# Retrieval in two rounds, and new places in memory for stationary and moving tiles, in a fused decoder block

## The chip, the cores and the metric

One NeuronCore of a Trainium2 chip runs the whole block as one program. The metric is the time of one execution on the device in microseconds (us); the kernel before takes 1010.98 us, the median of three runs (1010.77 to 1011.91).

## The reference, cut to what matters

256 tokens of width 1024 pass through one decoder layer: an attention part (a block-sparse and a latent branch, merged by gates), then a retrieval mixer (PEER), then a last norm. The change touches the mixer most. Per token and head (8 heads) it does this:

```
q  = (xc @ w_query)                      # 8 heads x 2 halves x 128
s1, s2 = q[:, :, 0] . sub_keys_1, q[:, :, 1] . sub_keys_2     # 128 scores each
v1, i1 = top_k(s1, 16);  v2, i2 = top_k(s2, 16)
cand = v1[..., :, None] + v2[..., None, :]                    # 256 sums
best, pos = top_k(cand, 16);  g = softmax(best)
idx = i1 * 128 + i2 at pos                                    # 16 of 16384 experts
act = gelu(expert_u[idx] . x);   out = sum(g * act * expert_v[idx])
```

The kernel gathers no experts. It multiplies every token with all 16384 rows of `expert_u` (128 groups of 128), multiplies the gelu of that by a matrix of gates that is zero except at the chosen experts, and multiplies the product with all of `expert_v`.

## The kernel before, in words

**Precision.** Every large product is made of three: a float32 operand is split into a rounded part `hi` and a rest `lo`, and TensorE adds hi*hi, hi*lo and lo*hi in PSUM. `emit_split` (lines 123 to 137) splits one weight unit of 128 x 1024: ScalarE writes `hi` (line 133), and GpSimd or VectorE subtracts for `lo` (line 135). Which of the two does so is fixed per unit in `lo_eng` (lines 107 to 110): GpSimd for the query weights and for the first NP = 8 expert groups, VectorE for all later ones. Weights arrive by DMAs of 512 KB on SyncE's queue, four buffers deep; `hi` and `lo` have four buffers each, and a unit is split two units ahead of its use.

**First stage, up to about 205 us.** `mm3` (lines 144 to 147) has activations as stationary operand and weights as moving one, 512 columns at a time in most steps. The stationary tiles are `hTh` and `hTl` (chunks 1 to 7 of the input projection, 4 units each, at 512 columns; chunk 0 has 416), `cTh` and `cTl`, the `yT` tiles (branch products) and `mTh` and `mTl` (output product). They lie in the pool `pb`, one tile after the other, each rounded up to 32 bytes. Byte addresses in a partition, divided by 128: `hTh` 954.75, `hTl` 1146.75, `mTh` 1082.75, `mTl` 1018.75, `cTh` 1236, `cTl` 1260, the four `yT` 1286 to 1382 (all even). The weight tiles `hi` and `lo` and the tiles `ah` and `al` of the last stage lie in other pools, all at odd whole numbers. `posi`, `posf` and `st` are small tiles of `pb` that stand ahead of these in the order of addresses (`posi` ahead of `hTh`, `posf` ahead of `cTh`, the four `st` ahead of the probability tiles `p` and `pt`).

**Queries and retrieval, about 205 to 365 us.** In 16 rounds `query(n)` makes a query half and `scores(n-1)` its 128 scores for both token halves; `top16` (lines 786 to 797) finds the 16 largest with VectorE's searches. From round 11 on, a generator (`retrieval`, lines 891 to 909) puts one piece of further work into VectorE's order at each call of `next(work)`. It treats four blocks (token half, head half) one after the other, each in full: sums of candidates (line 801), two searches of 80 candidates, `gate_in` and `decode`, `gate_exp` on ScalarE and `pick_keys` (lines 850 and 853, bf16 elements, 2048 of each partition), `gate_norm` and `fold_keys` (bf16 sums, line 858). When a block of the first token half is folded, `post` issues 64 indirect DMAs on GpSimd's queue that scatter its gates to DRAM. Between the calls `more_u(1)` puts one expert group (`u_block`, 24 matmuls of 256 columns, lines 737 to 739) into TensorE's order. Engines run their instructions in the order written.

**Wide expert steps, about 365 to 651 us.** `u_wide` (lines 747 to 754) does an expert group by 8 pairs: a matmul of 512 columns (`hi` against both parts of the activations, line 752) and one of 256 (`lo`, line 753). The activations are `h2`, with all blocks of the high part first and then all of the low part, so the 512 columns are two runs of 256 that lie 8 KB apart. Per pair of tokens a one-hot product (line 991) builds gates of the second token half. 35 groups are done narrow before this loop, 85 wide in it, and 8 narrow after it; results for the second token half are put into DRAM by `spill` until the gates are there.

**Last stage, 651 to 995 us.** Line 1075: the gated activations `ah` and `al` are stationary, the `expert_v` units move, 512 columns at a time.

Of the kernel before, what the change touches and what calls it, by code (L numbers as in the profile page):

```python
# [11 lines left out]
F32 = mybir.dt.float32  # L12
F32R = mybir.dt.float32r
BF = mybir.dt.bfloat16
U32 = mybir.dt.uint32
I32 = mybir.dt.int32
AF = mybir.ActivationFunctionType
OP = mybir.AluOpType
AX = mybir.AxisListType

P = 128
T = 256
NT = 2
D = 1024
ND = 8
H = 8
# [16 lines left out]
def block_kernel(ctx, tc, consts, constb, pos, x, g_mix, g_ffn, g_fin, w_in, g_q, w_qup, g_kv, w_kvup,  # L43
                 w_ba, w_bb, w_out, w_pq, keys, exp_u, exp_v, out):
    nc = tc.nc
    V, S, G, PE = nc.vector, nc.scalar, nc.gpsimd, nc.tensor
    ctx.enter_context(tc.manual_schedule())
    per = ctx.enter_context(tc.tile_pool(name="per", bufs=1))
# [104 lines left out]
    iota = per.tile([P, P, NB], BF, name="iota")  # L153
    small = per.tile([P, 64], F32, name="small")
    nc.gpsimd.memset(small[:, 63:64], -0.5)
    h2 = per.tile([P, 2, ND, T], F32R, name="h2")
    h2h, h2l = h2[:, 0], h2[:, 1]
    x2d = dram.tile([T, D], F32, name="x2d")
    gd = dram.tile([P * P * P, 1], F32, name="gd")
    gld = dram.tile([P, P, P], F32, name="gld")  # L160
# [40 lines left out]

    spread(0)
    idle(2)
    posi = pb.tile([P, NT], I32, name="posi")
    nc.gpsimd.dma_start(posi, pos)
    gqb = pb.tile([P, 384], F32, name="gqb")
    cb = pb.tile([P, B_I16], BF, name="cb")
# [118 lines left out]
        G.tensor_tensor(dst[:, :, half:], c3[:, :, half:], s3[:, :, :half], op=OP.add)  # L326


    posf = pb.tile([P, NT], F32, name="posf")
    G.tensor_copy(posf, posi)  # L330
    ang = pb.tile([P, NT, 48], F32, name="ang")
    kk = pb.tile([P, NT, 48], F32, name="kk")
# [149 lines left out]
    def att_a(i):  # L482
        q, k, v, h, sc, y = heads[i]
        s = sct()
        PE.matmul(s[:, :256], q[:, 128:], k, start=True, stop=False, skip_group_check=True)  # L485
        PE.matmul(s[:, 256:384], q[:, :128], k[:, :128], start=False, stop=False, skip_group_check=True)
        PE.matmul(s[:, 128:384], identb, maskb, start=False, stop=True, skip_group_check=True)
        st = pb.tile([P, 8], F32, name="st", tag="st", bufs=4)
        V.tensor_reduce(st[:, 0:1], s[:, 256:384], AX.X, OP.max)
        V.tensor_reduce(st[:, 1:2], s[:, :256], AX.X, OP.max)  # L490
        V.tensor_scalar(st[:, 2:4], st[:, 0:2], -sc, None, op0=OP.mult)
        p = pb.tile([P, 384], F32, name="p", tag="p", bufs=2)
        S.activation(p[:, :128], s[:, 256:384], AF.Exp, bias=st[:, 2:3], scale=sc, accum_out=st[:, 4:5])
        S.activation(p[:, 128:], s[:, :256], AF.Exp, bias=st[:, 3:4], scale=sc, accum_out=st[:, 5:6])
        live[i] = (p, st)
# [251 lines left out]
    def u_wide(j):  # L747
        hi, lo = wget(U_U[j])
        s = sct()
        for b in range(ND):  # L750
            bs = slice(b * P, (b + 1) * P)
            PE.matmul(s.rearrange("p (z n) -> p z n", z=2), hi[:, bs], h2[:, :, b, :], start=b == 0, stop=False)  # L752
            PE.matmul(s[:, :T], lo[:, bs], h2h[:, b, :], start=False, stop=b == ND - 1)  # L753
        return s

# [43 lines left out]
    def candidates(b):  # L799
        m, c = mval[b], cand[b]  # L800
        V.tensor_tensor(c[:, :, 0:16], m[:, 0, :, 0:1].to_broadcast([P, HG, 16]), m[:, 1], op=OP.add)
        V.tensor_tensor(c[:, :, 16:16 + 8 * NA].rearrange("p h (a b) -> p h a b", a=NA),
                        m[:, 0, :, 1:1 + NA, None].to_broadcast([P, HG, NA, 8]),
                        m[:, 1, :, None, 0:8].to_broadcast([P, HG, NA, 8]), op=OP.add)
        V.tensor_tensor(c[:, :, 16 + 8 * NA:], m[:, 0, :, 1 + NA:16],
                        m[:, 1, :, 0:1].to_broadcast([P, HG, 8]), op=OP.add)

    def retrieve_top(b, h):
        c, pos = cand[b], bpos[b]
        top16([(best[b][:, h + k, :], pos[:, h + k, :], c[:, h + k, :], rep[k][:, :NCAND]) for k in range(2)])  # L810
# [5 lines left out]
    def gate_in(b):  # L816
        V.tensor_tensor(gates(b).rearrange("p (h k) -> p h k", h=HG), best[b],
                        best[b][:, :, 0:1].to_broadcast([P, HG, 16]), op=OP.subtract)

    def gate_exp(b):  # L820
        S.activation(gates(b), gates(b), AF.Exp)

    def gate_norm(b):

        e = gates(b).rearrange("p (h k) -> p h k", h=HG)
        V.tensor_reduce(gsum, e, AX.X, OP.add)
        V.reciprocal(gsum, gsum)
        V.tensor_tensor(e, e, gsum[:, :, None].to_broadcast([P, HG, 16]), op=OP.mult)

    def decode(b):  # L830
        d = dec
        pf = bpos[b].rearrange("p h k -> p (h k)")
        V.tensor_copy(ix, midx[b].rearrange("p c h k -> p (c h k)")[:, :, None].to_broadcast([P, P, 2]))

        V.tensor_scalar(d[:, 0].bitcast(U32), pf, 3, None, op0=OP.logical_shift_right)
        V.tensor_scalar(d[:, 1].bitcast(U32), pf, 7, None, op0=OP.bitwise_and)
        V.tensor_copy(d[:, 4], pf)
        V.tensor_copy(d[:, 3], d[:, 0].bitcast(U32))
        V.tensor_copy(d[:, 5], d[:, 1].bitcast(U32))
        V.tensor_scalar(d[:, 0], d[:, 3], 1.0, 8.0, op0=OP.is_equal, op1=OP.mult)  # L840
        V.scalar_tensor_tensor(d[:, 5], d[:, 4], 15.5 + 8 * NA, d[:, 5], op0=OP.is_lt, op1=OP.mult)
        V.tensor_scalar(d[:, 3], d[:, 3], -1.0, 0.0, op0=OP.add, op1=OP.max)
        V.tensor_tensor(ab[:, 1].rearrange("p h k -> p (h k)"), d[:, 5], d[:, 0], op=OP.add)
        V.scalar_tensor_tensor(ab[:, 0].rearrange("p h k -> p (h k)"), d[:, 4], -float(8 + 8 * NA), d[:, 3],
                               op0=OP.add, op1=OP.max)

    def pick_keys(b):

        abv = ab.rearrange("p c h k -> p (c h) k")
        V.tensor_tensor(oh, abv[:, :, None, :].to_broadcast([P, H, 16, 16]),  # L850
                        i16b[:, None, :, :].to_broadcast([P, H, 16, 16]), op=OP.is_equal)
        o2 = oh.rearrange("p h a (k z) -> p (h a) k z", z=2)
        V.tensor_tensor(o2, o2, ix[:, :, None, :].to_broadcast([P, P, 8, 2]), op=OP.mult)

    def fold_keys(b):
        n = 8
        while n > 1:
            V.tensor_tensor(oh[:, :, :n], oh[:, :, :n], oh[:, :, n:2 * n], op=OP.add)  # L858
            n //= 2
        o4 = oh.rearrange("p (c h) a k -> p c h a k", c=2)  # L860
        t, g = b
        dst = sel[:, 0:2, g * 64:(g + 1) * 64] if t else ij
        V.tensor_tensor(dst.rearrange("p c (h k) -> p c h k", h=HG), o4[:, :, :, 0], o4[:, :, :, 1], op=OP.add)
        if t == 0:

            V.scalar_tensor_tensor(ij[:, 0], ij[:, 1], float(P), ij[:, 0], op0=OP.mult, op1=OP.add)
            V.tensor_scalar(addr[g], ij[:, 0], float(P), tok, op0=OP.mult, op1=OP.add)
# [4 lines left out]
    def post(g):  # L872


        for h in range(HG):
            own = []
            for k in range(16):
                c = slice(16 * h + k, 16 * h + k + 1)
                i = nc.gpsimd.indirect_dma_start(  # L879
                    out=gd[:, :], out_offset=bass.IndirectOffsetOnAxis(ap=addr[g][:, c], axis=0),  # L880
                    in_=gate[g][:, c], in_offset=None, compute_op=OP.add if g or h else OP.bypass).ins
                nc.gpsimd.nop()
                for m in own:
                    tc.declare_no_dep(i, m, reason="other experts")
                if k == 0:
                    for m in ends:
                        tc.add_manual_dep(i, m.name, SYNC, reason="same tokens, next head")
                own.append(i)
            ends[:] = own

    def retrieval(b):
        candidates(b)
        yield
        for h in range(0, HG, 2):
            retrieve_top(b, h)
            yield
        gate_in(b)
        decode(b)
        yield
        if b[0] == 0:  # L900
            gate_exp(b)
        pick_keys(b)
        yield
        if b[0] == 0:
            gate_norm(b)
        fold_keys(b)
        if b == (0, 1):
            post(1)
        yield

    def all_retrieval():
        for b in ((0, 0), (1, 0), (0, 1), (1, 1)):
            yield from retrieval(b)

    for n in range(2 * H):
        query(n)
        if n:
            scores(n - 1)
        if n == H + 2:
            work = all_retrieval()  # L920
        if n > H + 2:
            next(work)
    done = [0]

    def more_u(n):
        for _ in range(n):
            u_block(done[0])
            done[0] += 1

    more_u(1)  # L930
    next(work)
    scores(2 * H - 1)
    p2.close()

    while done[0] < NP - 2:
        more_u(1)
        next(work)
    post(0)

    def index_T():  # L940
        tr = trt()
# [7 lines left out]
        S.activation(gTh, tr[:, :P], AF.Copy)  # L949
        V.tensor_tensor(gTl, tr[:, :P], gTh.bitcast(F32), op=OP.subtract)  # L950

    while next(work, 0) is None:
        more_u(1 + done[0] % 2)
    for g in range(2):
        gate_exp((1, g))
        gate_norm((1, g))
    more_u(2)
    index_T()
    gate_T()
    more_u(1)  # L960
# [284 lines left out]
```

## Time and profile before

| | us |
|---|---|
| median of three runs (lowest, highest) | 1010.98 (1010.77, 1011.91) |
| the profiled execution | 1008.6 |
| its span, first to last instruction | 1006.8 |
| TensorE busy | 981.7 (98%) |
| TensorE loading weights | 851.4 (85%) |
| VectorE busy | 728.6 (72%) |
| ScalarE busy | 579.4 (58%) |
| GpSimd busy | 364.7 (36%) |

Busy times overlap. Matmuls are pipelined, so the duration of one is longer than the step from its start to the start of the next; the step is what the time is made of. The prediction's views are: the chain that ended last (followed back from the end, at each step to what released it), stretches with busy time and TensorE's granted clock, and instructions in order of time.

### The profile page before, as it was taken

The numbers are of one execution on the slowest core, as the hardware profiler recorded it, in microseconds if no ns is written. First come the engines' busy times: TensorE is split into PE (matmuls) and PEld (weight loads), VectorE is DVE, ScalarE is ACT, GpSimd is POOL, SyncE is SP. The second block draws the span as 40 slices with busy tenths as digits, with TensorE's granted clock in tenths as the row PEclk, the third lists the DMA queues.
The fourth block names the chain that finished last, engine by engine and source line by source line (L and its number), as shares of the span: only waits on it lengthen the run. The fifth ranks groups of instructions, "written<-read, shape, count | busy, mean of one in ns | idle before, by whom it ended". The sixth has DMA issues, their size and how long they took to land.

```text
span 1006.8 us, 16653 instructions
## 1 busy us (share of the span) xinstructions
PE 981.7 (98%) x5505; PEld 851.4 (85%) x5505; DVE 728.6 (72%) x1637; ACT 579.4 (58%) x1155; POOL 364.7 (36%) x247
## 2 busy tenths in 40 slices
PE   9999999999959999999999999999999999999997
PEld 6878888799959998888888888988888888888885
DVE  4745437657987768888888887677777777777775
ACT  4554463444525467887877877555555555555553
POOL 5645451177877787787778200000000000000000
PEclk9999999999979999999999999999999999999999
DMA  6854457454547888788888766698878888878773
GB/s 194 298 189 146 147 189 250 167 202 157 169 117 183 231 191 206 192 201 199 190 203 198 199 202 191 214 267 246 243 238 241 243 243 239 243 242 244 241 224 126
DMA packets 123096, 209.13 MB, mean 208 GB/s; under 512 B 28321, under 2 KB 75569, under 8 KB 122882
## 3 DMA queue, kind: packets, MB, share of 16 engines
q1 hardware_dynamic: 101232, 198.09, 63.6%
q0 software_dynamic: 16976, 0.96, 5.5%
q10 hardware_dynamic: 4802, 9.01, 2.4%
q8 instruction: 44, 0.72, 0.3%
q14 instruction: 42, 0.34, 0.1%
HBM read 189.59 MB, written 18.42 MB: 207 GB/s over the span
## 4 chain that ended last, share of the span: by engine, by line
PE 92%; DVE 5%; POOL 1%; issue 1%; ACT 1%; POOLq 0%; DVEq 0%; ACTq 0%
PE acc L1075 34%; PE sc L752 16%; PE sc L753 8%; PE acc L146 4%; PE acc L145 4%; PE acc L147 4%; PE sc L739 3%; PE sc L737 3%; PE sc L738 3%; PE acc L991 2%; PE sc L774 1%; PE sc L772 1%; PE sc L773 1%; DVE gm L858 1%; PE sc L485 1%
## 5 line engine op out<-in xcount | busy, mean ns | idle before, releaser
L135 DVE TENSOR_TENSOR lo<-raw,hi 128x1024 fp32r<-128x1024 f32 (+1 forms) x279 | 339.7, 1221 | 89.0 <-ACT hi L133 87.9
L133 ACT ACTIVATE hi<-raw 128x1024 fp32r<-128x1024 f32 (+2 forms) x323 | 339.0, 1053 | 12.7 <-PE acc L147 10.8
L752 PE MATMUL sc<-h,hi 128*128 128x512 f32 x680 | 243.2, 398 | 0.0
L879 POOL DMA_INDIRECT gd<-gate,addr x128 | 218.4, 1706 | 64.9 <-issue 36.6
L753 PE MATMUL sc<-h,lo 128*128 128x256 f32 x680 | 191.1, 281 | 0.0
L1126 POOL TENSOR_TENSOR small<-small 128x1 f32<-128x1 f32 x2 | 1.3, 646 | 440.0 <-DVE small L1124 440.0
L1075 PE MATMUL acc<-hi,al 128*128 128x512 f32 x512 | 157.9, 388 | 0.0
L1075 PE MATMUL acc<-lo,ah 128*128 128x512 f32 x512 | 157.8, 388 | 0.0
L1075 PE MATMUL acc<-hi,ah 128*128 128x512 f32 x512 | 157.7, 388 | 0.0
L752 PEld LDWEIGHTS sc<-h,hi 128*128 128x128 f32 x680 | 127.9, 188 | 28.8
L1059 ACT ACTIVATE ah<-gm 128x256 fp32r<-128x256 f32 x128 | 53.4, 418 | 155.8 <-DVE lo L135 147.8
L135 POOL TENSOR_TENSOR lo<-raw,hi 128x1024 fp32r<-128x1024 f32 x44 | 107.2, 2447 | 69.0 <-ACT hi L133 63.8
L753 PEld LDWEIGHTS sc<-h,lo 128*128 128x128 f32 x680 | 128.6, 189 | 0.0
L1075 PEld LDWEIGHTS acc<-hi,al 128*128 128x128 f32 x512 | 96.1, 188 | 19.9
L1075 PEld LDWEIGHTS acc<-lo,ah 128*128 128x128 f32 x512 | 96.1, 188 | 19.8
L1075 PEld LDWEIGHTS acc<-hi,ah 128*128 128x128 f32 x512 | 96.0, 188 | 19.8
L739 PE MATMUL sc<-h,lo 128*128 128x256 f32 x344 | 98.5, 286 | 10.9 <-DVE lo L135 10.9
L737 PE MATMUL sc<-h,hi 128*128 128x256 f32 x344 | 98.5, 286 | 0.0
L738 PE MATMUL sc<-h,hi 128*128 128x256 f32 x344 | 98.2, 286 | 0.0
L1060 DVE TENSOR_TENSOR al<-gm,ah 128x256 fp32r<-128x256 f32 x128 | 54.3, 424 | 56.2 <-ACT ah L1059 56.1
L739 PEld LDWEIGHTS sc<-h,lo 128*128 128x128 f32 x344 | 67.0, 195 | 11.2 <-DVE lo L135 11.1
L737 PEld LDWEIGHTS sc<-h,hi 128*128 128x128 f32 x344 | 67.0, 195 | 0.1
(266 smaller groups left out, 1503.4 us busy)
## 6 DMA issues: line engine op xcount, KB each, us to landing
raw<-in_exp_u_dram SPq DMA_DIRECT2D x128, 512.0 KB, 3.7
raw<-in_exp_v_dram SPq DMA_DIRECT2D x128, 512.0 KB, 4.7
raw<-in_w_in_dram SPq DMA_DIRECT2D x28, 512.0 KB, 3.6
gd<-zero ACTq DMA_DIRECT2D x8, 1024.0 KB, 5.6
raw<-in_w_pq_dram SPq DMA_DIRECT2D x16, 512.0 KB, 3.1
rl<-gd SPq DMA_DIRECT2D x128, 64.0 KB, 4.5
gld<-gs SPq DMA_DIRECT2D x120, 64.0 KB, 3.3
rl<-gld SPq DMA_DIRECT2D x120, 64.0 KB, 4.2
```

The lines of the kernel that those rows point to most:

```text
L133: S.activation(hi[:, :w], r[:, :w], AF.Copy)
L135: e.tensor_tensor(lo[:, :w], r[:, :w], hi[:, :w].bitcast(F32), op=OP.subtract)
L145: PE.matmul(o, sh, mh, start=start, stop=False)
L737: PE.matmul(so, hi[:, bs], h2h[:, b, :], start=b == 0, stop=False)
L738: PE.matmul(so, hi[:, bs], h2l[:, b, :], start=False, stop=False)
L739: PE.matmul(so, lo[:, bs], h2h[:, b, :], start=False, stop=b == ND - 1)
L752: PE.matmul(s.rearrange("p (z n) -> p z n", z=2), hi[:, bs], h2[:, :, b, :], start=b == 0, stop=False)
L753: PE.matmul(s[:, :T], lo[:, bs], h2h[:, b, :], start=False, stop=b == ND - 1)
L879: i = nc.gpsimd.indirect_dma_start(out=gd[:, :], out_offset=bass.IndirectOffsetOnAxis(ap=addr[g][:, c], axis=0), in_=gate[g][:, c], in_off ...
L1059: S.activation(ah, gm[:, j, :], AF.Copy)
L1060: V.tensor_tensor(al, gm[:, j, :], ah.bitcast(F32), op=OP.subtract)
L1075: PE.matmul(o, st[:, sl], mv[:, c:d], start=j == (0 if own is None else P - LAST) and mv is hi and st is ah, stop=j == P - 1 and st is al)
```

## The change

The retrieval is cut into two rounds. `find` goes through all four blocks with candidates, searches and `gate_in`; `read` then goes through them with `decode`, the comparison and the product of `pick_keys` as two pieces, and `gate_norm` with `fold_keys` (and `post`). All four `gate_exp` stand together, in the first block of `read`. An expert group is put behind each piece. The rounds take fewer groups, so 29 stand ahead of the loop of wide steps instead of 35, and 91 are wide instead of 85; the last six of these come behind the loop, where their gelu meets gates that are there, so they need no `spill`. `h2` is laid out block by block, high and low part side by side, and line 752 reads 512 columns in one run. Three small tiles are made larger (`posi` from 32 bytes with rounding to 64, `posf` from 32 to 128, each `st` from 32 to 64), by which the tiles behind them move: by 32 bytes from `hTh` on, by 128 from `cTh` on, by 256 from `p` on. The stationary tiles of the first stage then lie at odd multiples of 128 bytes (`hTh` 955, `mTh` 1083, `cTh` 1237, `yT` 1287 to 1383).

```diff
-    h2 = per.tile([P, 2, ND, T], F32R, name="h2")
-    h2h, h2l = h2[:, 0], h2[:, 1]
+    h2 = per.tile([P, ND, 2, T], F32R, name="h2")
+    h2h, h2l = h2[:, :, 0], h2[:, :, 1]
...
-    posi = pb.tile([P, NT], I32, name="posi")
+    posi = pb.tile([P, 16], I32, name="posi")[:, :NT]
...
-    posf = pb.tile([P, NT], F32, name="posf")
+    posf = pb.tile([P, 32], F32, name="posf")[:, :NT]
...
-        st = pb.tile([P, 8], F32, name="st", tag="st", bufs=4)
+        st = pb.tile([P, 16], F32, name="st", tag="st", bufs=4)
...
-            PE.matmul(s.rearrange("p (z n) -> p z n", z=2), hi[:, bs], h2[:, :, b, :], start=b == 0, stop=False)
+            PE.matmul(s, hi[:, bs], h2[:, b].rearrange("p z n -> p (z n)"), start=b == 0, stop=False)
...
-    def pick_keys(b):
+    def pick_keys(b, k):
-        V.tensor_tensor(oh, abv[:, :, None, :].to_broadcast([P, H, 16, 16]),
-                        i16b[:, None, :, :].to_broadcast([P, H, 16, 16]), op=OP.is_equal)
+        if k == 0:
+            V.tensor_tensor(oh, abv[:, :, None, :].to_broadcast([P, H, 16, 16]),
+                            i16b[:, None, :, :].to_broadcast([P, H, 16, 16]), op=OP.is_equal)
+            return
...
-    def retrieval(b):
...
-    def all_retrieval():
-        for b in ((0, 0), (1, 0), (0, 1), (1, 1)):
-            yield from retrieval(b)
+    BO = ((0, 0), (1, 0), (0, 1), (1, 1))
+    def find():
+        for b in BO:
+            candidates(b)
+            retrieve_top(b, 0)
+            yield
+            retrieve_top(b, 2)
+            gate_in(b)
+            yield
+    def read():
+        for b in BO:
+            decode(b)
+            yield
+            pick_keys(b, 0)
+            yield
+            if b == BO[0]:
+                for e in BO:
+                    gate_exp(e)
+            pick_keys(b, 1)
+            yield
+            gate_norm(b)
+            fold_keys(b)
+            if b[0] == 0:
+                post(b[1])
+            yield
+            yield
...
-            work = all_retrieval()
-        if n > H + 2:
+            work = find()
+        if n > H + 2 and n < 2 * H - 1:
             next(work)
...
     more_u(1)
-    next(work)
     scores(2 * H - 1)
     p2.close()
+    for _ in range(4):
+        more_u(1)
+        next(work)
     while done[0] < NP - 2:
         more_u(1)
-        next(work)
-    post(0)
+    for _ in read():
+        more_u(1)
...
-    while next(work, 0) is None:
-        more_u(1 + done[0] % 2)
-    for g in range(2):
-        gate_exp((1, g))
-        gate_norm((1, g))
-    more_u(2)
+    more_u(1)
     index_T()
     gate_T()
     more_u(1)
```

## Rows read from the trace of the kernel before

**Rows 1.** Page, part 4: the chain that ended last, by engine.

```profile
PE 92%; DVE 5%; POOL 1%; issue 1%; ACT 1%; POOLq 0%; DVEq 0%; ACTq 0%
```

**Rows 2.** Stretches: length, busy of PE, PEld, DVE, ACT, POOL; granted clock; DMA.

```profile
281.00:292.00 11.00, 0.45 (x4) 0.24 (x3) 10.73 (x53) 1.39 (x3) 8.26 (x10) 0.76 0.02 0
292.00:297.00 5.00, 4.67 (x22) 4.67 (x23) 4.93 (x22) 0.00 (x0) 4.07 (x4) 0.51 0.73 183
...
310.00:651.00 341.00, 341.00 (x2202) 309.14 (x2202) 274.99 (x604) 250.69 (x630) 195.79 (x111) 1.00 0.78 200
```

**Rows 3.** TensorE by time: start, duration (us), line; in brackets idle before.

```profile
280.33 0.28 PE L737 MATMUL sc<-h,hi 128*128 128x256 f32 x1
...
281.17 0.28 PE L738 MATMUL sc<-h,hi 128*128 128x256 f32 x1
292.33 0.58 PE L739 MATMUL sc<-h,lo 128*128 128x256 f32 x1 [10.88 <-DVE lo L135]
```

**Rows 4.** VectorE in order of time, from the search on (same columns).

```profile
246.70 1.10 DVE L801 TENSOR_TENSOR gm<-gm 128x64 f32<-128x64 f32 x1
...
248.13 0.48 DVE L789 MAX8 gm<-acc 128x8 f32<-128x128 f32 x2
...
250.50 0.36 DVE L789 MAX8 gm<-gm 128x8 f32<-128x80 f32 x2
...
252.34 0.47 DVE L789 MAX8 gm<-acc 128x8 f32<-128x128 f32 x2
...
258.90 0.21 DVE L817 TENSOR_TENSOR gate<-gm 128x64 f32<-128x64 f32 x1
...
260.40 0.49 DVE L789 MAX8 gm<-acc 128x8 f32<-128x128 f32 x2
```

**Rows 5.** VectorE in order of time, up to the first weight split.

```profile
264.01 3.32 DVE L853 TENSOR_TENSOR gm<-gm 128x2048 bf16<-128x2048 bf16 x1
...
269.62 7.87 DVE L858 TENSOR_TENSOR gm<-gm 128x1024 bf16<-128x1024 bf16 x3
...
280.66 0.20 DVE L801 TENSOR_TENSOR gm<-gm 128x64 f32<-128x64 f32 x1
...
291.06 1.22 DVE L135 TENSOR_TENSOR lo<-raw,hi 128x1024 fp32r<-128x1024 f32 x1
```

**Rows 6.** Line 853: duration ns min/median/max, first to last start.

```profile
L853 DVE TENSOR_TENSOR gm<-gm x4: 1225/1226/3323, 264.0 to 350.1; 128x2048 bf16<-128x2048 bf16 x4
```

**Rows 7.** VectorE in order of time, the third block of retrieval.

```profile
321.41 0.21 DVE L826 TENSOR_REDUCE small<-gate 128x4 f32<-128x64 f32 x1
...
324.33 1.22 DVE L135 TENSOR_TENSOR lo<-raw,hi 128x1024 fp32r<-128x1024 f32 x1
```

**Rows 8.** GpSimd in order of time.

```profile
263.13 14.21 POOL L135 TENSOR_TENSOR lo<-raw,hi 128x1024 fp32r<-128x1024 f32 x5 [0.30 <-ACT hi L133]
278.67 1.10 POOL L879 DMA_INDIRECT gd<-gate,addr  x1 [1.33 <-DVE gm L789]
...
558.31 2.30 POOL L879 DMA_INDIRECT gd<-gate,addr  x1 [0.31 <-issue]
```

**Rows 9.** TensorE in order of time, first chunks.

```profile
60.05 0.40 PE L147 MATMUL acc<-hi,hTl 128*128 128x512 f32 x1
...
65.65 0.40 PE L147 MATMUL acc<-hi,hTl 128*128 128x512 f32 x1
```

**Rows 10.** TensorE in order of time, wide expert steps.

```profile
426.77 0.40 PE L752 MATMUL sc<-h,hi 128*128 128x512 f32 x1
...
432.42 0.40 PE L991 MATMUL acc<-ow,oi 128*128 128x256 f32 x2
```

**Rows 11.** TensorE in order of time, second expert product.

```profile
699.94 0.61 PE L1075 MATMUL acc<-hi,ah 128*128 128x512 f32 x2
...
702.66 0.61 PE L1075 MATMUL acc<-hi,ah 128*128 128x512 f32 x2
```

**Rows 12.** Line 821 (columns as in group 6).

```profile
L821 ACT ACT_TABLE_LOAD  x2: 1283/1283/1283, 315.0 to 361.1; - x2
```

More of the change, by code (lines that the diff above doesn't have):

```diff
@@ L889, in post @@
             ends[:] = own
-    def retrieval(b):
[L892 to L895, printed above, removed]
-            yield
[L897 to L904, printed above, removed]
-            gate_norm(b)
[L906 to L909, printed above, removed]
-    def all_retrieval():
-        for b in ((0, 0), (1, 0), (0, 1), (1, 1)):
-            yield from retrieval(b)
+    BO = ((0, 0), (1, 0), (0, 1), (1, 1))
[3 more added lines that the diff above has]
+            retrieve_top(b, 0)
+            yield
+            retrieve_top(b, 2)
[12 more added lines that the diff above has]
+            yield
+            gate_norm(b)
+            fold_keys(b)
[3 more added lines that the diff above has]
+            yield
     for n in range(2 * H):
```

## The prediction

> **What bounds the kernel now.** The chain that ended last is 92% TensorE [rows 1]: nearly everywhere a matmul waits only for the matmul ahead of it. So time can come off in two ways: where TensorE stands still, or by a shorter step from one matmul to the next. The stretches show one place of the first kind. From 281 to 297 us TensorE ran only 4 + 22 matmuls [rows 2], while VectorE was busy throughout. In order of time, the matmul of line 739 at 292.33 us had stood 10.88 us, released by VectorE's split of the weights at line 135 [rows 3]. That split started at 291.06 us [rows 5], because VectorE runs its work in order and the retrieval of two blocks stood ahead of it. Two bf16 steps took most of that: the product at line 853 took 3.32 us and the three folds at line 858 took 7.87 us [rows 5], while over the whole run the median of line 853 is 1.23 us [rows 6]. At that time GpSimd was doing its last weight splits, five from 263.13 us on in 14.21 us [rows 8]. After the stop the granted clock was 0.51 from 292 to 297 us [rows 2], which is the lower of the two levels, 1.2 GHz; before and after TensorE was at 2.4.
>
> **The stop.** At full clock a 256-column step takes (281.17 - 280.33) / 7 = 0.12 us [rows 3], and an expert group of 24 takes 2.88 us. The 26 matmuls of the 16 us from 281 to 297 would need 3.1 us: 12.9 us are lost there, low clock included. That is what the first term can bring at most.
>
> What does the new order put ahead of that split? From 248.13 us on VectorE has five more rounds of scores at 2.37 us (248.13 to 250.50), eight searches at 1.84 us (250.50 to 252.34), three more sums of candidates, four `gate_in` and one `decode` (one of each takes 258.90 to 260.40, 1.50 us; three further `gate_in` 0.2 us each) [rows 4], and the split itself, 1.22 us [rows 5]. A sum of candidates takes 1.43 us beside a GpSimd split (246.70 to 248.13) [rows 4]; where line 801 takes 0.20 us [rows 5] instead of 1.10 it takes 0.53. Together 11.85 + 14.72 + 1.6 to 4.3 + 1.5 + 0.6 + 1.22 = 31.5 to 34.2 us: the split ends at 279.6 to 282.3 us. TensorE asks for it at 281.29, one step after 281.17 [rows 3]. So 0 to 1.0 us of stop is left; I take 0.5, as GpSimd splits beside two of the three sums.
>
> After that each block of `read` has 5 expert groups, 14.4 us of TensorE. VectorE's part is `decode` 1.4, lines 850 and 853 at 1.23 each (the first at the price of the second, same size), norm and fold 2.92 (321.41 to 324.33 [rows 7]), and five splits 6.1: 12.9 us. It fits, with 1.5 us to spare, as long as the bf16 work runs at its undisturbed price; GpSimd's splits end by 277.34 us [rows 8], before `read` begins. The first splits are due every 2.88 us, with at most 2.5 us of bf16 work and split between two of them, and 4.1 around the fold, behind which stands a group with no piece of its own. So the stop does not come back there.
>
> **Moved with it, at nothing.** ScalarE does four exponentials together: two table loads of 1.28 us [rows 12], some 3.6 us with the exponentials themselves. TensorE alternates between two score tiles, so ScalarE has 5.76 us for them and one group's gelu and rounding; without that cover up to 1 us would be lost. The 128 indirect DMAs on GpSimd's queue start some 10 us later; they ended at 560.6 us [rows 8], the first reader is at 651, so 90 us of cover become 80. On SyncE's queue six spills and six reloads of 64 KB go away. Inside the loop VectorE and ScalarE are busy 275 and 251 of 341 us [rows 2] and keep up with steps 2% shorter.
>
> **Stationary tiles.** Line 1075, whose stationary tiles lie at odd multiples of 128 bytes, steps 512 columns in (702.66 - 699.94) / 12 = 226.7 ns [rows 11]. In the first stage, with the same weight tiles moving but `hTh` at 954.75 times 128, it is (65.65 - 60.05) / 24 = 233.3 ns [rows 9]. At 2.4 GHz 512 columns are 213.3 ns. The difference of 6.6 ns I put down to the address, because that is what else differs for TensorE. It concerns 336 matmuls of chunks 1 to 7, 84 of the output product, 96 of the branches and 12 of line 447, in all 528: 3.5 us. Bounds: nothing, if the traffic of the first stage is the cause; the full 3.5; and below nothing 3.5 more, if the columns themselves get slower by as much. I take 3.5, the nearest row. The other matmuls that move (416, 384, 256 columns, transposes, attention) I leave at nothing. The first stage has no other bound to fall on, since the chain runs through TensorE [rows 1].
>
> The Trainium skill, "TensorE: Matmul & The Clock Gate", section "Back-to-back issue gap", gives the warm gap as N / 2.4 + 2.5 ns, 215.8 ns at 512 columns, with no term for the stationary tile's address or for a split run. By that rule this term and the next would be zero; the trace has 226.7 and 233.3 ns, above it in both places and not equal, so the rows decide.
>
> **The 512 columns in one run.** Sixteen pairs of lines 752 and 753 take 432.42 - 426.77 = 5.65 us, 353.1 ns each [rows 10]. With the 512-column step of line 1075, which reads one run, and the narrow step of 120 ns a pair would be 346.7 ns, 6.4 less. For the 85 groups that are wide already, 8 x 85 x 6.4 = 4.4 us. Six groups go from narrow, 2.88 us, to wide, 8 x 346.7 = 2.77: 0.6 more. Bounds of a pair: 341 (a further equal step down) and 360 (three narrow steps), which is +9 to -5 us; I take 346.7, built of two rows. Sum: 5.0.
>
> **Sum.** 12.9 - 0.5 + 3.5 + 5.0 = 20.9 us off the profiled execution's 1008.6, or 987.7. The median of the runs stands 2.4 us above that execution, so 990.
>
> **Rivals.** (1) The run of 512 columns is not the cause, and pairs of unequal length cost 353 ns as they are: 4.4 + 0.3 less gain, 995. For it: pairs exist nowhere else in the trace. Against: neither half alone has such a step. (2) The address does nothing: 3.5 less, 993.5. For it: the two rows are from different stages. (3) Both layout edits do nothing, the skill's rule: 998. (4) VectorE reaches the first splits some 3 us late, all searches at the price beside GpSimd, and the clock falls again (about 2 us as now: 5.0 less 22 x 0.12 less the 0.33 ahead of 292.33): 995; in the worst case the stop is only moved, and little is gained. (5) Slower: GpSimd's indirect DMAs, which now run beside three of the four blocks' bf16 work, slow it as its splits did. Price: line 853 costs 3.32 instead of 1.23 us, and norm with fold costs 280.66 - 267.33 - 2.37 (one round of scores) = 10.96 instead of 2.92 [rows 4 to 7], 10.1 us more per block. Less the 1.5 to spare, that is 8.6 us of stop in each of three blocks, with some 2 us at low clock after each: 32 us lost against 20.9, 1022. It decides from 6.5 us lost per block. Against it: only one of four executions of line 853 took 3.32 us; the others, from 288 to 350 us, took 1.23 [rows 6], while indirect DMAs were issued from 278.67 to 558.31 us [rows 8].
>
> The rule of the skill for that, "SBUF — State Buffer", section "Who interferes with whom", is that a VectorE instruction with two inputs in SBUF contends with a GpSimd instruction that reads SBUF. The trace agrees for splits (3.32 against 1.23 us) and not for the indirect DMAs.
>
> **Chances and range.** Forecast 0.56, rival 1 0.13, rival 2 0.11, rival 3 0.06, rival 4 0.09 (0.02 of it with nothing gained), rival 5 0.05. A measurement can tell 0.2%, about 2 us, from no change. Faster: 0.93; same: 0.02; slower: 0.05. The range goes from 986 (pairs at 341 ns, no stop left) to 997, over rivals 1, 2 and most of 4; rivals 3 and 5 stay out, 0.11.
>
> **What would show it.** Right: no wait of TensorE over 1 us between 250 and 320 us; granted clock 1.0 there; line 853 at 1.23 us four times; first-stage steps at 227 ns; pairs at 347 ns; line 1075 unchanged. Wrong: VectorE's split of the ninth group after 282 us; a step of 233 ns with `hTh` at 955; pairs at 353.

## The result, and the profile after

| | before | after |
|---|---|---|
| median (us) | 1011.16 | 998.46 (998.02 to 998.95) |
| profiled execution, its span | 1008.6, 1006.8 | 998.02, 996.2 |
| forecast | | 990 (986 to 997) |

The ratio is 0.9878 with a 95% interval of 0.9865 to 0.9891: faster by 12.7 us, where 21 were forecast. The median before is that of four runs here; the three that stand ahead of the prediction gave 1010.98. On one of the other chips that the experiments ran on, the same kernel gained 0.4% only (last experiments).

The chain that ended last in the kernel after, by engine, answers to [rows 1] and is again TensorE:

```profile
PE 91%; DVE 5%; issue 1%; ACT 1%; POOL 1%; DMA 0%; POOLq 0%; DVEq 0%; ACTq 0%
```

The stretches of [rows 2] in the kernel after (length, busy of PE, PEld, DVE, ACT, POOL; granted clock, DMA share, GB/s):

```profile
281.00:292.00 11.00, 9.12 (x63) 9.12 (x64) 10.51 (x22) 7.00 (x13) 0.92 (x1) 0.84 0.56 162
292.00:297.00 5.00, 5.00 (x44) 5.00 (x43) 4.63 (x14) 2.44 (x6) 3.78 (x5) 1.00 0.92 246
310.00:651.00 341.00, 341.00 (x2116) 305.39 (x2115) 277.62 (x586) 249.88 (x631) 202.62 (x116) 1.00 0.81 200
```

TensorE ran 107 matmuls in the first two stretches, where it ran 26. The stop of 10.88 us [rows 3] is now one of 2.15, and it waits for the same line. TensorE in order of time, kernel after:

```profile
280.46 0.28 PE L739 MATMUL sc<-h,hi 128*128 128x256 f32 x1
282.88 0.38 PE L740 MATMUL sc<-h,lo 128*128 128x256 f32 x1 [2.15 <-DVE lo L135]
```

VectorE in order of time, kernel after, answers to [rows 4, 5]: two small operations of 64 elements beside GpSimd's splits, one without, and the first weight split of VectorE.

```profile
268.61 1.48 DVE L802 TENSOR_TENSOR gm<-gm 128x64 f32<-128x64 f32 x1
...
274.23 1.62 DVE L818 TENSOR_TENSOR gate<-gm 128x64 f32<-128x64 f32 x1
275.77 0.21 DVE L802 TENSOR_TENSOR gm<-gm 128x64 f32<-128x64 f32 x1
...
281.61 1.22 DVE L135 TENSOR_TENSOR lo<-raw,hi 128x1024 fp32r<-128x1024 f32 x1
```

GpSimd's last split, beside the second of them, and line 856 (line 853 before, [rows 6]; duration min/median/max in ns):

```profile
273.37 2.40 POOL L135 TENSOR_TENSOR lo<-raw,hi 128x1024 fp32r<-128x1024 f32 x1 [0.48 <-ACT hi L133]
```

```profile
L856 DVE TENSOR_TENSOR gm<-gm x4: 1219/1219/1220, 285.0 to 327.3; 128x2048 bf16<-128x2048 bf16 x4
```

All four products take 1.22 us now, none 3.32. So the bf16 work did move out of GpSimd's way.

TensorE's steps in the kernel after: first chunks, 24 steps [rows 9]; wide steps, sixteen pairs [rows 10]; last stage, twelve steps [rows 11].

```profile
60.15 0.39 PE L147 MATMUL acc<-hi,hTl 128*128 128x512 f32 x1
...
65.59 0.39 PE L147 MATMUL acc<-hi,hTl 128*128 128x512 f32 x1
...
423.56 0.40 PE L753 MATMUL sc<-h,hi 128*128 128x512 f32 x1
...
429.22 0.40 PE L998 MATMUL acc<-ow,oi 128*128 128x256 f32 x2
...
690.10 0.61 PE L1082 MATMUL acc<-lo,ah 128*128 128x512 f32 x2
...
692.82 0.39 PE L1082 MATMUL acc<-lo,ah 128*128 128x512 f32 x1
```

The first gives 5.44 / 24 = 226.7 ns, 6.6 less than before, as forecast. The second gives 5.66 us for sixteen pairs, where it was 5.65: nothing. The third is unchanged at 226.7.

The account, from the starts of the same matmuls in both traces (us):

| | forecast | measured |
|---|---|---|
| expert groups ahead of the wide loop (the stop) | -12.4 | -9.46 |
| start to the transposes of the mixer's input (addresses) | -3.5 | -1.52 |
| wide loop, and six groups made wide (one run) | -5.0 | -0.31 |
| transposes to the first query (clock) | 0 | +0.95 |
| the rest | 0 | -0.24 |
| span | -20.9 | -10.58 |

In the first row the six groups that are wide now are taken out at 6 x 2.88 us; in the third they count with what a wide group saves. The transposes are those of `hg`, the normalised input of the mixer, which close the first stage. The other 2.1 of the 12.7 us are where the profiled executions lie: 2.56 below the median before, 0.44 after.

The clock's 0.95: the granted clock of the stretch from 195 to 205 us was 1.00 in the kernel before,

```profile
195.00:205.00 10.00, 7.23 (x50) 5.27 (x48) 7.20 (x13) 4.37 (x11) 1.85 (x2) 1.00 0.14 54
```

and lower in the kernel after:

```profile
195.00:205.00 10.00, 7.13 (x35) 4.80 (x35) 5.75 (x13) 4.97 (x10) 1.27 (x2) 0.83 0.17 59
```

TensorE waits 2.3 us near 198 us in both. In some executions it then gets the lower level, 1.2 GHz, for 3.4 us, in some it doesn't; the one profiled before did not.

### The profile page after: what moved, and what is told of

Its sections match the earlier page's. It is cut to its first block, busy times and chain, and to the rows that moved or that the text cites. A ratio compares the mean times of both kernels' runs of the same rounds, so it can differ in the third digit from the quotient of the medians.

```text
span 996.2 us, 16542 instructions
## 1 busy us (share of the span) xinstructions
PE 980.0 (98%) x5456; PEld 849.7 (85%) x5457; DVE 725.8 (73%) x1649; ACT 578.9 (58%) x1159; POOL 361.4 (36%) x247
## 4 chain that ended last, share of the span: by engine, by line
PE 91%; DVE 5%; issue 1%; ACT 1%; POOL 1%; DMA 0%; POOLq 0%; DVEq 0%; ACTq 0%
PE acc L1082 35%; PE sc L753 17%; PE sc L754 9%; PE acc L146 4%; PE acc L145 4%; PE acc L147 4%; PE sc L740 3%; PE sc L739 3%; PE sc L738 3%; PE acc L998 2%; PE sc L774 1%; PE sc L773 1%; PE sc L775 1%; PE sc L486 1%; DVE gm L794 1%
## 5 line engine op out<-in xcount | busy, mean ns | idle before, releaser
L753 PE MATMUL sc<-h,hi 128*128 128x512 f32 x728 | 260.1, 398 | 0.0
L753 PEld LDWEIGHTS sc<-h,hi 128*128 128x128 f32 x728 | 136.9, 188 | 30.8
L135 POOL TENSOR_TENSOR lo<-raw,hi 128x1024 fp32r<-128x1024 f32 x44 | 105.1, 2393 | 70.2 <-ACT hi L133 69.8
L738 PE MATMUL sc<-h,hi 128*128 128x256 f32 x296 | 84.7, 286 | 0.0
L739 PE MATMUL sc<-h,hi 128*128 128x256 f32 x296 | 84.4, 285 | 0.0
L759 ACT ACTIVATE us<-sc 128x256 f32<-128x256 f32 x91 | 35.1, 385 | 59.2 <-PE sc L754 59.2
```

Of the source, the lines that this page charges most:

```text
L135: e.tensor_tensor(lo[:, :w], r[:, :w], hi[:, :w].bitcast(F32), op=OP.subtract)
L738: PE.matmul(so, hi[:, bs], h2h[:, b, :], start=b == 0, stop=False)
L739: PE.matmul(so, hi[:, bs], h2l[:, b, :], start=False, stop=False)
L753: PE.matmul(s, hi[:, bs], h2[:, b].rearrange("p z n -> p (z n)"), start=b == 0, stop=False)
```

## Experiments: the wide pairs

Theory: with 512 and 256 columns in turn, the change of length costs (rival 1). Against it: the two runs cost, and something else hid the gain. The first kernel has the new order and addresses, but the old layout of `h2`.

```diff
-    h2 = per.tile([P, ND, 2, T], F32R, name="h2")
+    h2 = per.tile([P, 2, ND, T], F32R, name="h2")
...
-            PE.matmul(s, hi[:, bs], h2[:, b].rearrange("p z n -> p (z n)"), start=b == 0, stop=False)
+            PE.matmul(s.rearrange("p (z n) -> p z n", z=2), hi[:, bs], h2[:, :, b, :], start=b == 0, stop=False)
```

> The changed kernel with the old layout of h2 again (two runs of 256 columns 8 KB apart); addresses and retrieval stay as changed. Theory A: the step of a pair, 353 ns before and after the change, is set by the two lengths that alternate, and the layout is worth nothing: pairs of 353 ns, the loop of wide steps 255.0 us long, time 998.5 within 1 us. Theory B: one run helps, but something else in the changed kernel took it back in the same steps: pairs slower than 353 ns, about 360, and the time 4 to 5 us above 998.5.

997.43 us (995.97 to 998.57), ratio 0.9868 [0.9849, 0.9887], and the loop from the first to the last one-hot product takes 252.68 us, as with one run (and as in the kernel before). Sixteen pairs of this kernel take 5.66 us, as in the changed one:

```profile
424.11 0.40 PE L753 MATMUL sc<-h,hi 128*128 128x512 f32 x1
...
429.77 0.40 PE L998 MATMUL acc<-ow,oi 128*128 128x256 f32 x2
```

The layout brings nothing. The second kernel keeps the new layout and puts equal lengths together:

```diff
             PE.matmul(s, hi[:, bs], h2[:, b].rearrange("p z n -> p (z n)"), start=b == 0, stop=False)
+        for b in range(ND):
+            bs = slice(b * P, (b + 1) * P)
             PE.matmul(s[:, :T], lo[:, bs], h2h[:, b, :], start=False, stop=b == ND - 1)
```

> The changed kernel, with the eight 512-column matmuls of a wide step first and then the eight 256-column ones, instead of pairs. Theory A (alternating lengths keep the step from settling at the columns plus 13 ns): 512 columns step at 227 ns and 256 at 120, a wide step takes 2.77 instead of 2.83 us, 91 of them 4.7 us less, 994. Theory B (the pair's cost comes from what is read: same tiles, same addresses, same number of columns): 236 and 117 ns as in pairs, 998.5.

995.29 us (995.06 to 995.46), ratio 0.9852 [0.9835, 0.9869]; the loop takes 249.88, 2.8 us less. TensorE in order of time, this kernel:

```profile
425.65 2.00 PE L753 MATMUL sc<-h,hi 128*128 128x512 f32 x8
427.49 1.12 PE L756 MATMUL sc<-h,lo 128*128 128x256 f32 x8
428.44 0.40 PE L1000 MATMUL acc<-ow,oi 128*128 128x256 f32 x2
```

Eight steps of 512 take 1.84 us, 230 each, and eight of 256 take 0.95. By their place in the row of eight (means over all 91 wide groups, ns to the next start):

```
512 columns: 233.3 235.9 228.3 232.5 230.9 226.7 226.7 226.7
256 columns: 113.3 119.1 120.0 120.0 120.0 120.0 120.0 120.0
```

The step settles at the 226.7 and 120 ns of which the forecast built its pair, but at 226.7 only from the sixth on. So a change of length costs, and in turns it is paid at each pair: 353.3 ns instead of 346.7. Grouped, a pair still takes 349.2 on average, so the 91 groups gave 3.0 us of the 4.7 expected. That `hi` and `lo` alternate as stationary tiles is not the cause: they do so in the narrow groups too, where 256-column steps are settled at 120 ns. Both together, old layout and equal lengths:

> The changed kernel with equal lengths one after the other in a wide step (eight of 512 columns, then eight of 256) and with the old layout of h2, so that each 512 are two runs 8 KB apart. Theory A (lengths and addresses set the step, the number of runs does nothing): steps of 230.6 and 118.9 ns as with one run, the loop of wide steps 249.9 us. Rival (one run does help once lengths are equal): 512 columns at 233 ns or more, the loop 252 us or more.

One profiled execution: 996.23 us, loop 249.88 again. With settled lengths too, two runs cost what one does.

## Experiments: the stationary tiles

The small tiles get their old sizes back, all else stays:

```diff
-    posi = pb.tile([P, 16], I32, name="posi")[:, :NT]
+    posi = pb.tile([P, NT], I32, name="posi")
...
-    posf = pb.tile([P, 32], F32, name="posf")[:, :NT]
+    posf = pb.tile([P, NT], F32, name="posf")
...
-        st = pb.tile([P, 16], F32, name="st", tag="st", bufs=4)
+        st = pb.tile([P, 8], F32, name="st", tag="st", bufs=4)
```

> The changed kernel without the three larger small tiles: the stationary tiles of the first stage are back at their old addresses, all else as changed. Theory A (the address sets the step): 512-column steps of the first stage back at 233 ns from 227 to 230, about 500 of them, 1.5 to 2 us more, 1000.3. Rival: the steps became shorter for another reason (what else ran then): 227 to 230 ns stay and the time is 998.5.

999.74 us (997.77 to 1001.05). TensorE in order of time, this kernel, 24 steps in (65.89 - 60.28) = 5.61 us, 233.8 ns:

```profile
60.28 0.39 PE L147 MATMUL acc<-hi,hTl 128*128 128x512 f32 x1
...
65.89 0.39 PE L147 MATMUL acc<-hi,hTl 128*128 128x512 f32 x1
```

The stage up to the transposes takes 195.19 us against 193.44, but its start differs by more than that from one execution to the next, mostly by when the granted clock rises for good (between 15 and 21 us). From a matmul near 42 us on, the traces agree: from there to the transposes the four with the old addresses take 153.28 to 153.29 us, the sixteen with the new ones 151.44 to 151.53. So the addresses bring 1.8 us; the account's 1.52 has 0.3 of the start against it. The other way round, an unused tile of 128 bytes moves `ah` and `al` to even multiples of 128 bytes:

```diff
     vp = ctx.enter_context(tc.tile_pool(name="vp", bufs=6))
+    vp.tile([P, 32], F32, name="shift", bufs=1)
```

> The changed kernel with an unused tile of 128 bytes ahead of the gated activations of the last stage, so that its stationary tiles lie at even multiples of 128 bytes; nothing else differs. Theory A (the address alone sets the step): the 512-column steps of the last stage go from 226.7 to some 232 ns, as those with the even tiles of the first stage had, and 1500 of them make it 8 us slower, 1006.5. Rival: addresses do not matter where the last stage is concerned, 226.7 ns stay, 998.5.

1005.66 us (1005.51 to 1008.44), ratio 0.9964 [0.9948, 0.9981]: the last stage takes 356.86 us instead of 348.18. Twelve of its steps take 2.79 us, 232.5 ns each:

```profile
700.37 0.63 PE L1083 MATMUL acc<-hi,al 128*128 128x512 f32 x2
...
703.16 0.39 PE L1083 MATMUL acc<-hi,al 128*128 128x512 f32 x1
```

The address does it, in both directions and in two stages.

## Experiments: what is left of the stop, and the low clock

Can the 2.15 us be had? One kernel puts the last two searches behind the seventh group, so the split comes ahead of them:

```diff
-    for _ in range(4):
+    for _ in range(3):
...
-    while done[0] < NP - 2:
+    while done[0] < NP - 1:
         more_u(1)
+    next(work)
+    more_u(1)
```

> The changed kernel with the last two searches moved behind the seventh expert group, and one more group ahead of the second round, so that VectorE's first weight split stands ahead of those searches (31 narrow groups, 89 wide). Theory (the stop of 2.3 us and the low clock after it are this split's lateness alone): no wait over 0.4 us between 275 and 300 us, no low clock after it, 4 us less: 994.5. Rival (the lateness only moves to the next split): a stop of 1 to 2 us some 3 us later, and 997 or more.

997.62 us (996.97 to 998.5), ratio 0.9854 [0.9828, 0.9879]. From 275 to 290 us TensorE is busy all 15 us at clock 1.00, so the stop is gone (columns as above):

```profile
275.00:290.00 15.00, 15.00 (x128) 15.00 (x127) 13.77 (x54) 8.96 (x20) 1.06 (x1) 1.00 0.63 201
```

But two new waits of 0.6 us stand at 317.7 and 319.1, and the 994.5 that was expected is missed. The other kernel lets GpSimd split three more groups (`range(NP + 3)` where `lo_eng` is filled), which takes the late split off VectorE and puts the contention back:

> The changed kernel with the splits of three more expert groups (the ninth to the eleventh) on GpSimd instead of VectorE; they then run beside the bf16 work of the first block. Theory (GpSimd's splits slow VectorE's bf16 sums, as before the change): the bf16 product of the first block again takes 2.4 to 3.3 us instead of 1.22, while it takes 1.22 in the other three blocks; but no stop at the ninth group, since GpSimd splits it by 278.5 us: about 995. Rival (the slow bf16 steps of the kernel before had another cause): 1.22 us in all four blocks.

998.98 us (998.14 to 1000.37). Line 856, then VectorE and GpSimd in order of time, this kernel:

```profile
L856 DVE TENSOR_TENSOR gm<-gm x4: 1218/1220/3305, 285.4 to 329.9; 128x2048 bf16<-128x2048 bf16 x4
...
285.41 3.31 DVE L856 TENSOR_TENSOR gm<-gm 128x2048 bf16<-128x2048 bf16 x1
...
285.16 2.47 POOL L135 TENSOR_TENSOR lo<-raw,hi 128x1024 fp32r<-128x1024 f32 x1 [2.49 <-ACT hi L133]
```

The one product that runs beside a split takes 3.31 us, the other three 1.22. That is the prediction's reading of the old stop, shown by putting it back, and what the Trainium skill, "SBUF — State Buffer", section "Who interferes with whom", states: a VectorE instruction with two inputs in SBUF contends with a GpSimd instruction that reads SBUF; these rows agree. The stop at 280 us is gone, and one of 2.1 us stands at 290.5, behind the fold; so the 995 that was expected is missed.

For the low clock at 201 us, 18 instead of 9 filling matmuls (`idle(18)`):

> The changed kernel with 18 instead of 9 matmuls on zeros where TensorE waits for the last norm of the first stage, about 198 us. Theory (the low clock from 201.4 to 204.8 us follows from that wait of 2.3 us): no low clock there, 1 to 1.5 us less, 997. Rival (the clock falls for another reason, or matmuls on zeros do not hold it): low clock there as before, 998.5, or more if the added matmuls delay the transposes.

999.53 us (998.4 to 1001.25): no gain in time. Its stretch from 195 to 205 us:

```profile
195.00:205.00 10.00, 9.14 (x59) 6.12 (x58) 7.28 (x14) 4.26 (x11) 2.29 (x2) 1.00 0.14 54
```

Here the clock is 1.00 and transposes to first query take 8.96 us instead of 9.85. That does not show that the fill did it: five profiled executions with nine matmuls took 8.9 to 9.0 us as well (8.91 with the old sizes of the small tiles). And this kernel, too, had new waits after 312 us, and a low clock from 317.6 on.

## Experiments: a stop that one chip has and another has not

Four of these kernels ran on a second chip, where the kernel before takes 1012.1 us: old layout with equal lengths, later searches, more splits on GpSimd, 18 filling matmuls. All four had new waits of TensorE between 312 and 320 us; the four on the first chip had none. So the changed kernel ran again, on a third chip, beside three others.

> The changed kernel once more, on the chip of this call. If the wait of 1 to 2 us at 312 to 319 us that four kernels of the call before showed belongs to the chip: it shows here too when that chip is drawn, and then 1 to 2 us above 998.5. If it belongs to the edits of those four kernels: none here, and 998 to 999.

1010.59 us (1010.05 to 1011.18, six runs), ratio 0.9964 [0.9952, 0.9976]; the kernel before takes 1013.59 there. The stretches from 296 to 321 us, this run (columns as above):

```profile
296.00:301.00 5.00, 5.00 (x44) 5.00 (x43) 3.43 (x4) 1.39 (x3) 3.95 (x4) 1.00 0.59 201
301.00:306.00 5.00, 1.48 (x10) 1.01 (x9) 0.17 (x1) 0.60 (x3) 3.83 (x4) 0.86 0.32 105
306.00:311.00 5.00, 3.09 (x11) 2.75 (x12) 3.37 (x8) 0.78 (x1) 3.87 (x4) 0.50 0.39 120
311.00:316.00 5.00, 2.35 (x10) 2.24 (x10) 0.00 (x0) 0.00 (x0) 2.56 (x3) 0.50 0.01 0
316.00:321.00 5.00, 5.00 (x35) 4.94 (x34) 3.34 (x10) 3.13 (x9) 4.09 (x4) 0.77 0.45 66
```

In these 25 us the groups lose all that the run loses: they take 100.93 us instead of 88.25. The clock at 0.50 is the lower level, 1.2 GHz, after TensorE stood from 302.8 on. ScalarE and TensorE in order of time, same run:

```profile
305.39 0.28 ACT L722 ACTIVATE gm<-sc 128x128 f32<-128x128 f32 x1 [6.62 <-remote]
316.18 0.28 ACT L722 ACTIVATE gm<-sc 128x128 f32<-128x128 f32 x1 [9.40 <-remote]
```

```profile
305.89 0.58 PE L738 MATMUL sc<-h,hi 128*128 128x256 f32 x1 [3.13 <-remote]
...
310.37 0.37 PE L739 MATMUL sc<-h,hi 128*128 128x256 f32 x1 [1.04 <-issue]
311.08 0.37 PE L740 MATMUL sc<-h,lo 128*128 128x256 f32 x1 [0.34 <-issue]
312.49 0.37 PE L738 MATMUL sc<-h,hi 128*128 128x256 f32 x1 [1.04 <-issue]
```

TensorE stands between matmuls of one group, whose data are there, with no release that the profile shows ("issue"); ScalarE stands for 6.62 and 9.40 us, and VectorE and SyncE wait for ScalarE. The other work that runs at that time is GpSimd's: its indirect DMAs began at 291.47 us. The prediction had them as rival 5, as contention with VectorE. VectorE's own instructions keep their 1.22 us here, so if the DMAs are the cause, it is by another way.

The trace's records say more. Both of ScalarE's waits end 0.02 us behind TensorE's signal that a group is done (305.37 and 316.16 us). These signals come 6.2 and 13.4 us behind the last matmul recorded for their groups, and that of the group before 1.1 us; in the other 26 narrow groups it is 0.02 at most. And records of landed DMAs are missing, just while the indirect DMAs run: up to 291 us this trace has 1796, that of the same kernel on the fourth chip below 1795; from 291 to 600 us it has 3626 against 5213. All eight traces from the two chips with new waits have 11,724 to 11,898 in all, those of the changed kernel and its variants with all DMAs on chips without them 13,211 to 13,265. That points to the indirect DMAs, on these chips. It does not show them as the cause, nor whether the recording of the trace has a part in it. Late loads of instructions are not seen: the last 16 KB load ahead of the stop starts at 296.8 us and takes 0.94, on the fourth chip at 296.7 and 0.95.

The three beside it: the order of the retrieval alone, on the kernel before with its layout and its addresses,

```diff
-            work = all_retrieval()
+            work = find()
...
+    for _ in read():
+        more_u(1)
```

> The kernel before with the new order of the retrieval alone: old layout of h2 (two runs), old addresses of the small tiles. If the order is nearly the whole gain: 9 to 10 us below the kernel before, so 1000 to 1002, and within 1.5 us above the changed kernel with the old addresses alone (999.7). If the layout of h2 had brought something that the runs so far do not show: above 1002.

Two of ten runs took 999.7 and 1000.8 us, eight 1009.2 to 1013.8 (median of the ten 1012.24). Where the stop stays short, in the profiled execution (999.73) two waits of 1.1 and 0.6 us, the order alone is nearly the whole gain, as expected; in most runs on this chip it is lost again. The last two kernels join the lengths in groups to the later searches; the second of them fills with 18 matmuls:

> The changed kernel with two edits that each gained something alone: the eight 512-column matmuls of a wide group ahead of its eight 256-column ones, and the last two pieces of the search round behind the seventh group (31 groups narrow). If the two gains add up: from the changed kernel's 998.5, 2.8 to 3.2 us by the lengths and 0.8 us by the searches, 994.5 to 995; if the wait near 318 us stays away as well, up to 3 us more, about 992. If the searches only move the stop, 995.3 as with the lengths alone. No stop near 280 us in either case.

> The same with 18 instead of 9 matmuls that fill TensorE's wait near 198 us. If the low clock at 201 us in the changed kernel follows from that wait: none there, and the stretch from the transposes of the gates to the first query 0.9 us shorter, so 0.5 to 1 us below the kernel without this edit. If the filling matmuls delay the work behind them by as much as they save: no difference, within 0.5 us.

997.44 us (992.13 to 998.48) and 996.35 (993.86 to 997.41), ratios 0.9827 [0.9803, 0.9851] and 0.9819 [0.9803, 0.9834]: 13 to 14 us faster than the changed kernel on the same chip. Most of that is the long stop, which none of their ten runs has; the 994.5 to 995 that was expected is missed. Their waits between 314 and 321 us add up to some 2.5 and 3.6 us, so both have the short form of the stop. So the chip alone does not make the long one: it depends on the program too. Whether the fill helps, these intervals don't tell. In the profiles the stretch from the transposes to the first query took 8.98 instead of 9.86 us with it, which kernels with nine matmuls reach too.

Do the indirect DMAs cause the stop? Four kernels on a fourth chip, two on a fifth:

```diff
-            if b[0] == 0:
-                post(b[1])
```

> The changed kernel once more, beside the next three on one chip. Where the stop at 301 to 315 us of the run before shows: about 1010; where it doesn't: 998 to 999; with a short form of it, as in four earlier kernels: 1000 to 1001.

> The changed kernel without the 128 indirect DMAs of GpSimd; the gates of the first token half stay zero, so half of the mixer's output is left out. Theory A, the stop at 301 to 315 us comes from the indirect DMAs: no such stop on any chip, no wait of TensorE or ScalarE over 0.5 us from 290 to 330 us, 995 to 999, and below the changed kernel of this call by whatever stop that one has. Theory B, it belongs to the chip or to the place of the program: the stop stays, and the time is that of the changed kernel within 1 us.

> The changed kernel with all indirect DMAs behind the last piece of the read round, so they begin at about 345 us instead of 291. Theory A: no stop at 301 to 315 us, and one of the same kind 10 to 24 us after the new beginning, at 355 to 370 us, in the wide steps; the DMAs end near 635 us, before the last stage reads. If what stops is only the narrow steps, with their more frequent instructions: no stop at either place, 996 to 999 on every chip. Theory B: the stop stays at 301 to 315 us.

> The kernel before, for its profile on this chip. Its indirect DMAs begin at 279 us, beside VectorE's stop of TensorE from 281 to 292 us. Theory A: a stop of the same kind lies at 290 to 305 us, partly under the stop that is there, so on a chip where the changed kernel loses 12 us this kernel loses 1 to 4 us against its 1011. If the kernel before has nothing of the kind: 1011 on every chip.

> The changed kernel on one more chip: about 1010 with the stop at 301 to 315 us, 1000 to 1001 with a short form of it, 998 to 999 without; the kernel before then stands at 1013 to 1014, 1012, or 1010 to 1011, as on the four chips before.

> The changed kernel without the 128 indirect DMAs of GpSimd (half of the mixer's output is left out), beside the changed kernel on one chip. Theory A, the stop at 301 to 315 us comes from the indirect DMAs: 996 to 999 and no wait of TensorE over 0.5 us from 290 to 330 us, also where the changed kernel stands at 1010. Theory B, it belongs to the chip: the time of the changed kernel within 1 us. Where the changed kernel has no stop on this chip, the run can't tell the two apart.

Neither chip had the stop: the changed kernel took 998.39 and 997.69 us there, without the DMAs 997.92 and 997.87. So they cost nothing where there is no stop, and whether they cause it stays open. The late version took 998.0 and did not do what I meant: GpSimd has nothing else in its queue and starts as soon as the addresses are there, wherever the program has the DMAs. GpSimd, kernel with the DMAs put later:

```profile
290.13 1.26 POOL L882 DMA_INDIRECT gd<-gate,addr  x1 [15.30 <-ACT gs L724]
```

The kernel before took 1009.94 on the fourth chip. Its stop was that of [rows 3] and nothing more:

```profile
293.07 0.58 PE L739 MATMUL sc<-h,lo 128*128 128x256 f32 x1 [10.90 <-DVE lo L135]
```

Whether it has the new stop on the third chip, no trace shows; its 1013.59 us there are 2 to 4 more than on the chips without the stop, which is what theory A expects.

## Why the prediction was wrong

The range ended at 997 and the median is 998.46. The span falls 10.3 us short of the sum; by its steps:

**The 512 columns in one run**: the failed step, 4.7 of the 10.3. Of 5.0 us came 0.31, the six groups made wide. The prediction put the 6.4 ns of a pair down to the two runs; the kernels with runs apart and with equal lengths together show that they belong to the change of length. The step took the price of a 512-column matmul from a row where all neighbours have 512 columns, and of a 256-column one from a row of 256s, and no row in which they alternate was compared with those. Rival 1 said this and gave 995. The formula of the Trainium skill ("TensorE: Matmul & The Clock Gate", section "Back-to-back issue gap") gives 215.8 and 109.2 ns; the section means it for a single matmul by itself, names 131 ns at 512 columns for a stream of weight loads and matmuls, and has no term for the length of the neighbours. The settled steps here are 226.7 and 120, so no run agrees with either.

**The stop**: right in kind, 2.9 us too large. The split starts at 281.61 and ends at 282.8, just after the interval of 279.6 to 282.3. The 0.5 us of stop that I took stood for an end at 281.8. One more operation fell beside a GpSimd split than I had counted: `gate_in` at 274.23 took 1.62 us, priced at 0.2. TensorE also asked 0.7 us sooner than put, at 280.58, and VectorE began its list only 0.5 us sooner. And behind a stop of 2.15 us came 3.4 us at the lower clock, for which the sum had nothing. The groups lost 4.7 us in all against 14.2 before.

**Stationary tiles**: the mechanism is right, by both address kernels, and mis-sized: 1.5 us in the account (1.8 where the start is left out), not 3.5. The long chunks step in 226.7 ns. But where other matmuls come between, in the attention part, the 512-column steps take some 230 behind them: the same settling that the kernel with equal lengths shows. The forecast took 6.6 ns for all 528.

**At nothing**: the exponentials with their table loads, the spills and the later indirect DMAs cost nothing on the chip of the result, as put: behind the stop of 2.15 us TensorE has no further wait of 0.1 us or more. The clock at 201 us, 0.95, was not in the sum; the row of before had it at 1.00 by chance of that execution. The same holds for the 2.4 us added from execution to median, of which only 0.4 were due after.

**Rivals.** The first is what happened, on most chips, and a part of the fourth: VectorE reached the split late, by 1 us instead of 3, and the clock fell again. The range took the rivals one at a time; three misses of 4.7, 2.9 and 2.0 us together lie beyond it. The fifth gave 1022 by contention with VectorE, which no run shows; the stop on the third chip lies at the same place and takes back 12.1 us, by a way that stays open.

## What to carry to other kernels

Put matmuls of equal length next to each other, and price a step from a row with the same neighbours; nearly half of the missing gain was a step taken out of its company. Stationary tiles at odd multiples of 128 bytes are worth looking at wherever a stage is a long row of 512-column matmuls. Where several terms can each fall short, let the range hold two of them at once. And where a change shortens a stop that work on another queue ran beside, time it on more than one chip.

## What the runs showed of the hardware that was not expected

- A 512-column step needs five others of its length before it settles: 233.3, 235.9, 228.3, 232.5, 230.9, then 226.7 ns; a 256-column step is shorter at first (113.3, 119.1, then 120.0).
- Two runs that lie 8 KB apart cost a moving operand nothing (252.68 us both ways, 249.88 both ways).
- The stationary tile's address moves the 512-column step from 226.7 to 232.5 ns at even multiples of 128 bytes (last stage), and to 233.3 to 233.8 at 954.75 times 128 (first stage).
- One program on one core took 998.5 us in the result, 998.4 and 997.7 on two further chips of the experiments, and 1010.6 on another, in all six runs there. There TensorE's signals to ScalarE came up to 13.4 us behind its recorded matmuls, and records of landed DMAs are missing while GpSimd's indirect DMAs run; the cause stays open.
